# Moving a kernel's own DRAM traffic from SyncE's queue to GpSimd's, in a two-layer hybrid encoder

## The chip, the cores and the metric

The kernel runs on one core of a Trainium2 chip. A core has the engines TensorE (PE, its weight loads PEld), VectorE (DVE), ScalarE (ACT), GpSimd (POOL) and SyncE (SP), and sixteen DMA engines that move data between DRAM and the on-chip memory. Each engine works its own instruction list in order and waits on semaphores for the others; a DMA is issued by an instruction on one engine and runs on the DMA engines. The metric is the device time of one execution in microseconds, as the median of several runs.

## The reference

Two layers run over 256 tokens of 1024 channels (float32). Cut to what matters:

```python
h = rmsnorm(x, norm1_g[l])
rq, rk, rv, rg, c_q, c_kv, k_rope, s5_u, gate_logits = split(h @ w_in[l])
y_ret = retention(rq, rk, rv, rg)              # A: 4 heads, both directions
y_mla = latent_attention(c_q, c_kv, k_rope)    # B: 8 heads, softmax over 256 keys
y_s5  = glu(gelu(s5(s5_u) + d * s5_u) @ w_glu) # C: 64 groups x 64 complex states, both directions
proj  = einsum('bsnk,nkd->bsnd', stack(y_ret, y_mla, y_s5), w_branch[l])
x = x + sum(sigmoid(gate_logits) * proj) @ w_out[l]
x = x + (silu(f_gate) * f_up) @ ffn_w_down[l]  # f_gate, f_up from rmsnorm(x) @ ffn_w_gu[l]
```

After the second layer there is a final RMSNorm.

## The kernel before, in words

Activations are held with channels on the partitions. A dense product takes its weights as tiles `raw` of up to 128 x 1024 numbers, 512 KB each, out of five buffers (`wraw`). ScalarE rounds each into `wh` (L668), VectorE takes the rest `wl` = `raw` - `wh` (L669), and TensorE makes three matmuls for each 128-row block (L673, L674, L675; L713 to L715 for the GLU). Some of the first products use `raw` as it is (L725).

The S5 branch is a generator (`s5`) that runs in the background of the dense work: after each weight tile, `tick` gives it some credit, and it emits a few steps. The order in which the engines execute is then set by a planner which takes instructions from each engine's list by priority, once their inputs are ready by its own estimate of times. So the place of an instruction on an engine depends on how long the planner thinks that earlier DMAs take.

On-chip memory is short, and so the kernel keeps much of its own data in DRAM (tiles from the pool `dr`) and fetches it again: the powers `pxd`, the input factors `bbd`, sixteen state tables `wtd` in layer 1, transposed inputs and states `utd`, `sfd`, `sbd`, some gates `gd`, the skip term `dud`, the residual `xd`. One use is more than storage. In `s5_out` a product of 128 x 480 numbers, `kf`, is stored to `kd`, and four loads read it back as overlapping windows of 128 (steps of 16 numbers), one load of 128 KB for each group `g4`, into the tile `M` (tag `wt`, two buffers). This happens once for every two values of the loop's `qq`, eight times in a layer. Here it is called a round: ScalarE copies `kf` (L598), a store, four loads, then the matmuls of L629 in `s5_emit`, which take `M` as weights. `s5_emit` comes one step later in the program than the store (`delay`=1).

All of these transfers, like the loads of weights and inputs, go through one helper, `dma` (L121), which issues them on SyncE. GpSimd has only memsets: the last 16 columns of the tile `t_bb` (L365), two columns of the state tiles (L472, L473), parts of other tiles.

Of the kernel before, what the change touches and what calls it, by code (L numbers as in the profile page):

```python
# [78 lines left out]
class Kern:  # L79
# [40 lines left out]
    def dma(self, out, src, pin=False):  # L120
        i = self.nc.sync.dma_start(out, src)  # L121
        if self.pin or pin:
            self.tc.keep_in_program_order(i)
        return i

    def s4(self, dt=F32):
        return self.s(1024, "s4", dt=dt)
# [161 lines left out]
    def s5_tables(self, l):  # L289


        nc, V, A = self.nc, self.nc.vector, self.nc.scalar
        pn, cf = yield from self.s5_params(l)
        yield 4.0
        PX = self.s4().rearrange("p (j d g) -> p j d g", j=8, d=2)
        for b in range(2):
            ps = self.bank(self.p5)
            for j in range(4):
                nc.tensor.matmul(ps[:, j * P:(j + 1) * P], pn[:, b * 4 + j].rearrange("p r q -> p (r q)"),
                                 self.perm, start=True, stop=True)  # L300
            A.copy(PX[:, b * 4:b * 4 + 4].rearrange("p j d g -> p (j d g)"), ps)
        CF = self.s(2 * 64, "t_cf").rearrange("p (r g) -> p r g", r=2)
        ps = self.bank(self.p5)
        nc.tensor.matmul(ps[:, 0:P], cf.rearrange("p r q -> p (r q)"), self.perm, start=True, stop=True)
        for r in range(2):
            for d in range(2):
                A.copy(CF[d * 64:d * 64 + 64, r, :], ps[r * 64:r * 64 + 64, d * 64:d * 64 + 64])
        PW = self.s4().rearrange("p (r s g) -> p r s g", r=2, s=8)
        A8 = self.s(2 * 64, "t_a8").rearrange("p (r g) -> p r g", r=2)
        A8s = self.s(2 * 64, "t_a8s").rearrange("p (r g) -> p r g", r=2)  # L310
        for r in range(2):
            nc.gpsimd.memset(PW[0:64, r, 0, :], 1.0 - r)
            nc.gpsimd.memset(PW[64:128, r, 7, :], 1.0 - r)
            rows = slice(r * 64, r * 64 + 64)
            A.copy(PW[0:64, r, 1:8, :], PX[rows, 0:7, 0, :])
            A.copy(PW[64:128, r, 6::-1, :], PX[rows, 0:7, 1, :])
        for d in range(2):
            rows = slice(d * 64, d * 64 + 64)
            A.copy(A8[rows, 0, :], PX[0:64, 7, d, :])
            A.copy(A8[rows, 1, :], PX[0:64, 7, d, :])  # L320
            A.mul(A8s[rows, 0, :], PX[64:128, 7, d, :], -1.0)
            A.copy(A8s[rows, 1, :], PX[64:128, 7, d, :])
        PXD = self.t(self.dr, [P, 1024], "pxd", 2)
        self.dma(PXD, PX.rearrange("p j d g -> p (j d g)"))
        if l == 0 and self.nl >= 0:
            while "b" not in self.cx:
                yield None
            br, bi = self.cx.pop("b")
        else:
            br, bi = self.s4(), self.s4()  # L330
            for f in self.load_b(l, br, bi):
                f()
        BB = [self.s4(), self.s4()]
        for qh in range(2):
            c = slice(qh * 512, qh * 512 + 512)
            nat = lambda t: t[:, c].rearrange("p (h q c) -> p h q c", h=4, q=8)
            natt = lambda t: t.rearrange("p (h q c) -> p h q c", h=4, q=8)
            cfv = lambda r: (CF[:, r, qh * 32:qh * 32 + 32].rearrange("p (q h) -> p h q", h=4)
                             .unsqueeze(3).to_broadcast([P, 4, 8, GC]))
            for r, (x, y, op) in enumerate(((br, bi, ALU.subtract), (bi, br, ALU.add))):  # L340
                yield 1.9
                t1, t2 = self.s(512, "tm"), self.s(512, "tm")
                V.tensor_tensor(natt(t1), cfv(0), nat(x), ALU.mult)
                V.tensor_tensor(natt(t2), cfv(1), nat(y), ALU.mult)
                V.tensor_tensor(BB[r][:, c].rearrange("p (q h c) -> p h q c", q=8, h=4), natt(t1), natt(t2), op)
        BBD = self.t(self.dr, [P, 2048], "bbd", 2)
        for r in range(2):
            self.dma(BBD[:, r * 1024:(r + 1) * 1024], BB[r])
        PD = self.s(512, "t_pd").rearrange("p (s g) -> p s g", s=8)
        V.tensor_tensor(PD, PW[:, 1], PW[:, 0], ALU.subtract)  # L350
        V.scalar_tensor_tensor(PW[:, 1], PW[:, 1], -1.0, PW[:, 0], ALU.mult, ALU.subtract)
        BS = self.s4()
        V.tensor_tensor(BS, BB[0], BB[1], ALU.add)
        return dict(PW=[PW[:, 0], PW[:, 1], PD], PXD=PXD, A8=A8, A8s=A8s, BB=[BS, BB[1], BB[0]], BBD=BBD)

    def s5_out_tables(self, l, tb, qh):
# [3 lines left out]
        BB2 = self.s(2 * 528, "t_bb2", 1).rearrange("p (d x) -> p d x", d=2)  # L360
        for d in range(2):
            for r in range(2):
                self.dma(BB2[r * 64:r * 64 + 64, d, 0:512],
                                  tb["BBD"][d * 64:d * 64 + 64, r * 1024 + qh * 512:r * 1024 + qh * 512 + 512])
            nc.gpsimd.memset(BB2[:, d, 512:528], 0.0)  # L365
        AB = self.s4().rearrange("p (k d j g) -> p k d j g", k=2, d=2, j=8)
        gs = slice(qh * 32, qh * 32 + 32)
        PX = self.s(512, "ev").rearrange("p (j d g) -> p j d g", j=8, d=2)
        self.dma(PX, tb["PXD"].rearrange("p (j d g) -> p j d g", j=8, d=2)[:, :, :, gs])
        gs = slice(0, 32)  # L370
        for d in range(2):
            js = slice(0, 8) if d == 0 else slice(7, None, -1)
# [27 lines left out]
    def s5(self, l, ctx, gel_out):  # L400
# [4 lines left out]
        wtd = None  # L405
        if l > 0:
            wtd = []
            for qq in range(16):
                wt = yield from self.s5_wt(tb, qq)
                d = self.t(self.dr, [P, 1024], "wtd", 16)  # L410
                self.dma(d, wt)
                wtd.append(d)
                yield self.yw / 2 if self.fw else self.yw
            tb.pop("PW"), tb.pop("BB")
# [26 lines left out]
        for qq in range(16):  # L441
            if wtd is None:
                wt = yield from self.s5_wt(tb, qq)
            else:
                wt = self.s(1024, "wt")
                self.dma(wt, wtd[qq])
            WT = wt.rearrange("p (g r x) -> p g r x", g=4, r=2)
            if qq % 2 == 0:
                pl = self.bank(self.p5)
# [51 lines left out]
        for t, k in ((UT, "utd"), (Sf, "sfd"), (Sb, "sbd")):  # L501
            d = self.t(self.dr, [P, 1024], k, 2)
            v = t.pop()
            self.dma(d, v if len(v.shape) == 2 else v.rearrange("p a b -> p (a b)"))
            t.append(d)
        del v
        tb.update(UT=UT, Sf=Sf, Sb=Sb)
# [33 lines left out]
    def s5_out(self, l, tb, du_load, gel_out):  # L541
        nc, V, A, T = self.nc, self.nc.vector, self.nc.scalar, self.nc.tensor
        pend = todo = None
        for qq in range(16):
            qh, q = qq // 8, qq % 8
            if q == 0:
                BB2, C1, C2, AB = yield from self.s5_out_tables(l, tb, qh)
                yq = self.s4().rearrange("p (t q c) -> p t q c", t=8, q=8)
                UT, Sf, Sb = (tb[k][qh] for k in ("UT", "Sf", "Sb"))
                if qh:  # L550
                    ts = []
                    for d in (UT, Sf, Sb):
                        t = self.s4()
                        self.dma(t, d)
                        ts.append(t)
                    UT = ts[0].rearrange("p (q x) -> p q x", q=8)
                    Sf, Sb = (t.rearrange("p (g n) -> p g n", n=32) for t in ts[1:])
                yield 1.0
# [38 lines left out]
            kf = self.s(512, "ev")[:, 0:480]  # L597
            A.copy(kf, pk[:, 0:480])  # L598
            kd = self.t(self.dr, [P, 480], "kd", 4)
            self.dma(kd, kf)  # L600
            M = self.s(1024, "wt").rearrange("p (h q m) -> p h q m", h=4, q=2)
            for g4 in range(4):
                base = kd[g4 * 32:g4 * 32 + 16, :]
                src = bass.AP(tensor=base.tensor, offset=base.offset, ap=[[16, 8], [480, 16], [240, 2], [1, 128]])
                self.dma(M[:, g4].rearrange("p q m -> p (q m)"), src)
            job = (list(pend), M, po, yq, UT, Sf, Sb, qh, q)
            pend = None
            if self.delay:
# [567 lines left out]
    def gate(self, l, n, h, c):  # L1176
        th = self.s(512, "ev")
        if (n, c) in self.gd:
            self.dma(th, self.gd.pop((n, c)))
            return th  # L1180
        pg = yield from self.pair_steps(self.a["w_in"][l], OFF_GATE + n * D + c * 256, h.get)
        self.nc.scalar.activation(th, pg, AF.Tanh, scale=0.5)
# [2 lines left out]
    def early_gates(self, l, h, ns):  # L1185

        for n, c in ns:
# [1 line left out]
                continue  # L1189
            th = yield from self.gate(l, n, h, c)  # L1190
            self.gd[n, c] = self.t(self.dr, [P, 512], "gd", 12)
            self.dma(self.gd[n, c], th)

    def branch(self, l, n, y, c):
        return self.pair_steps(self.a["w_branch"][l, n], c * 256, y.get)
# [1 line left out]
    def layer(self, l, x2, acc, xg, last):  # L1197
# [28 lines left out]
        for qh in range(2):  # L1226
# [11 lines left out]
                                 scale=sd[:, k:k + 1])  # L1238
            dus.append(du)
            if not (l == 0 and self.nl >= 0):  # L1240
                self.dma(dud[:, qh * 1024:(qh + 1) * 1024], du)
        while self.loads:
            self.load()
        if l == 0 and self.nl >= 0:
            for qh in range(2):
                self.dma(dud[:, qh * 1024:(qh + 1) * 1024], dus[qh])
        del du, dus
        xd = self.t(self.dr, [P, 2048], "xd", 1)
        for i in range(2):
            self.dma(xd[:, i * 1024:(i + 1) * 1024], x2[i])  # L1250
        cx = self.cx
        gel = []

        def du_load(qh):
            t = self.s4()
            self.dma(t, dud[:, qh * 1024:(qh + 1) * 1024])
            return t

        def gel_out(qh, y):
# [65 lines left out]
        acc = self.squares(2 * S)  # L1325
        x2 = [self.s4(), self.s4()]
        for i in range(2):
            self.dma(x2[i], xd[:, i * 1024:(i + 1) * 1024])
        g2 = self.vec["norm2_g"][l]
        h2 = self.hl(2)  # L1330
        for c in range(4):
# [168 lines left out]
```

## Time and profile before

| | |
|---|---|
| median of 3 runs | 1427.78 us (1423.44 to 1439.42) |
| profiled execution, its time | 1425.45 us |
| profiled execution, its span | 1423.5 us |
| mean granted clock of TensorE | 0.982 |
| PE, DVE, ACT, POOL busy | 94%, 73%, 57%, 0% of the span |
| DMA, read and written | 231.53 MB and 27.53 MB |

The profile is one execution. The span goes from the first to the last instruction; the time has 1.95 us more around it. The three runs lie within 16 us, 1.1% of the median.

### The profile page before, as it was taken

The numbers are of one execution on the slowest core, as the hardware profiler recorded it, in microseconds if no ns is written. First come the engines' busy times: TensorE is split into PE (matmuls) and PEld (weight loads), VectorE is DVE, ScalarE is ACT, GpSimd is POOL, SyncE is SP. The second block draws the span as 40 slices with busy tenths as digits, with TensorE's granted clock in tenths as the row PEclk, the third lists the DMA queues.
The fourth block names the chain that finished last, engine by engine and source line by source line (L and its number), as shares of the span: only waits on it lengthen the run. The fifth ranks groups of instructions, "written<-read, shape, count | busy, mean of one in ns | idle before, by whom it ended". The sixth has DMA issues, their size and how long they took to land.

```text
span 1423.5 us, 27613 instructions
## 1 busy us (share of the span) xinstructions
PE 1334.4 (94%) x11102; PEld 1234.2 (87%) x11102; DVE 1042.3 (73%) x1910; ACT 807.0 (57%) x1339; POOL 4.5 (0%) x33
## 2 busy tenths in 40 slices
PE   7899998888999999999999999788999999999997
PEld 5866878867888999999999868778988899999997
DVE  7977867877687679988668547877768657777754
ACT  3656576974654455545446677786564344544442
POOL 0000000000000000000000000000000000000000
PEclk9999999999999999999999999999999999999999
DMA  8944233646786699766679784365687667666662
GB/s 218 250 146 118 69 104 99 182 137 152 211 219 194 201 211 260 210 199 197 188 229 273 239 267 131 99 193 156 157 247 188 193 200 204 181 185 187 179 179 79
DMA packets 433891, 260.84 MB, mean 183 GB/s; under 512 B 61714, under 2 KB 413284, under 8 KB 433764
## 3 DMA queue, kind: packets, MB, share of 16 engines
q1 hardware_dynamic: 433764, 259.09, 64.3%
q8 instruction: 87, 1.43, 0.4%
q14 instruction: 40, 0.33, 0.1%
HBM read 231.53 MB, written 27.53 MB: 182 GB/s over the span
## 4 chain that ended last, share of the span: by engine, by line
PE 68%; ACT 13%; DMA 8%; DVE 6%; issue 3%; SPq 1%; DVEq 0%; ACTq 0%
PE pw L673 17%; PE pw L674 17%; PE pw L675 17%; DMA wt<-kd 3%; ACT wh L668 3%; PE pw L713 2%; PE pw L714 2%; PE pw L715 2%; DVE wl L669 2%; DMA kd<-ev 2%; ACT s L497 2%; PE p L536 2%; PE p L452 2%; DMA raw<-in_w_in 1%; SPq L121 1%
## 5 line engine op out<-in xcount | busy, mean ns | idle before, releaser
L673 PE MATMUL pw<-s,wh 128*128 128x256 f32 x2472 | 714.6, 290 | 16.6 <-ACT wh L668 13.8
L675 PE MATMUL pw<-s,wl 128*128 128x256 f32 x2472 | 703.5, 285 | 8.4 <-DVE wl L669 8.3
L674 PE MATMUL pw<-s,wh 128*128 128x256 f32 x2472 | 703.0, 285 | 0.2 <-DVE s L749 0.2
L668 ACT CAST wh<-raw 128x1024 fp32r<-128x1024 f32 (+4 forms) x394 | 381.0, 972 | 456.2 <-PE pw L674 290.7
L669 DVE TENSOR_TENSOR wl<-raw,wh 128x1024 fp32r<-128x1024 f32 (+4 forms) x394 | 443.1, 1128 | 206.8 <-ACT wh L668 205.4
L673 PEld LDWEIGHTS pw<-s,wh 128*128 128x128 f32 x2472 | 472.1, 191 | 34.1 <-ACT wh L668 16.6
L675 PEld LDWEIGHTS pw<-s,wl 128*128 128x128 f32 x2472 | 472.5, 191 | 15.5 <-DVE wl L669 11.2
L674 PEld LDWEIGHTS pw<-s,wh 128*128 128x128 f32 x2472 | 472.9, 191 | 6.6 <-issue 4.8
L713 PE MATMUL pw<-s,wh 128*128 128x256 f32 x256 | 71.9, 281 | 0.0
L714 PE MATMUL pw<-s,wh 128*128 128x256 f32 x256 | 71.9, 281 | 0.0
L715 PE MATMUL pw<-s,wl 128*128 128x256 f32 x256 | 71.9, 281 | 0.0
L569 DVE TENSOR_TENSOR wy<-s,s 128x512 f32<-128x512 f32 x64 | 42.3, 687 | 16.1 <-PE pa L629 10.3
L715 PEld LDWEIGHTS pw<-s,wl 128*128 128x128 f32 x256 | 48.2, 188 | 0.0
L714 PEld LDWEIGHTS pw<-s,wh 128*128 128x128 f32 x256 | 48.2, 188 | 0.0
L713 PEld LDWEIGHTS pw<-s,wh 128*128 128x128 f32 x256 | 48.2, 188 | 0.0
L536 PE MATMUL p<-ident,wy 128*128 128x128 f32 x256 | 36.7, 276 | 11.5 <-ACT s L468 11.1
L497 ACT COPY s<-s 64x256 f32<-64x256 f32 (+1 forms) x64 | 40.7, 636 | 5.2 <-DVE s L483 4.3
L536 PEld LDWEIGHTS p<-ident,wy 128*128 128x128 f32 x256 | 28.6, 140 | 16.6 <-ACT s L468 13.2
L570 DVE TENSOR_TENSOR tm<-s,s 128x512 f32<-128x512 f32 x64 | 43.0, 687 | 0.0
L571 DVE TENSOR_TENSOR wy<-wy,tm 128x512 f32<-128x512 f32 x64 | 42.7, 685 | 0.0
L748 ACT ACTIVATE s<-ev 128x512 fp32r<-128x512 f32 x46 | 29.1, 633 | 19.7 <-DVE ev L1350 12.1
L531 DVE TENSOR_TENSOR wy<-wy,tm 128x1024 f32<-128x1024 f32 x32 | 39.1, 1221 | 0.3
(284 smaller groups left out, 1549.7 us busy)
## 6 DMA issues: line engine op xcount, KB each, us to landing
raw<-in_w_in SPq DMA_DIRECT2D x122, 512.0 KB
raw<-in_ffn_w_gu SPq DMA_DIRECT2D x88, 512.0 KB
raw<-in_w_branch SPq DMA_DIRECT2D x48, 512.0 KB
raw<-in_s_w_glu SPq DMA_DIRECT2D x32, 512.0 KB
raw<-in_ffn_w_down SPq DMA_DIRECT2D x32, 512.0 KB
wt<-kd SPq DMA_DIRECT2D x64, 128.0 KB
raw<-in_w_out SPq DMA_DIRECT2D x16, 512.0 KB
wtd<-wt SPq DMA_DIRECT2D x16, 512.0 KB
```

The lines of the kernel that those rows point to most:

```text
L497: A.copy(*todo.pop(0))
L536: T.transpose(ps[:, i * P:(i + 1) * P], W[i % 2][:, gp * 2 + i // 2].rearrange("p s c -> p (s c)"), self.ident)
L570: V.tensor_tensor(t2, tv(1), cv(C2), ALU.mult)
L571: V.tensor_tensor(y[:, :, js, :], y[:, :, js, :], t2, ALU.add)
L668: self.nc.scalar.copy(hi, src)
L669: self.nc.vector.tensor_tensor(lo, src, hi.bitcast(F32), ALU.subtract)
L673: T.matmul(ps, lh, rh, start=first, stop=False)
L674: T.matmul(ps, lh, rl, start=False, stop=False)
L675: T.matmul(ps, ll, rh, start=False, stop=last)
L713: T.matmul(o, wh[:, k, c], xh, start=(half == 0 and m == 0 and k == 0), stop=(k == 3), **f)
L714: T.matmul(o, wh[:, k, c], xl, start=False, stop=(k == 3), **f)
L715: T.matmul(o, wl[:, k, c], xh, start=False, stop=(k == 3), **f)
```

## The change

A new helper `park` issues a transfer on GpSimd's queue. Every store of the kernel's own data to DRAM and every load of it back calls `park` in place of `dma`. Loads of inputs, weights and constant tables, and the stores of the output, stay with `dma` on SyncE. The tiles, their buffers and the compute instructions are the same.

```diff
+    def park(self, out, src):
+
+        return self.nc.gpsimd.dma_start(out, src)
...
-        self.dma(PXD, PX.rearrange("p j d g -> p (j d g)"))
+        self.park(PXD, PX.rearrange("p j d g -> p (j d g)"))
...
-            self.dma(BBD[:, r * 1024:(r + 1) * 1024], BB[r])
+            self.park(BBD[:, r * 1024:(r + 1) * 1024], BB[r])
...
-                self.dma(BB2[r * 64:r * 64 + 64, d, 0:512],
+                self.park(BB2[r * 64:r * 64 + 64, d, 0:512],
                                   tb["BBD"][d * 64:d * 64 + 64, r * 1024 + qh * 512:r * 1024 + qh * 512 + 512])
...
-        self.dma(PX, tb["PXD"].rearrange("p (j d g) -> p j d g", j=8, d=2)[:, :, :, gs])
+        self.park(PX, tb["PXD"].rearrange("p (j d g) -> p j d g", j=8, d=2)[:, :, :, gs])
...
-                self.dma(d, wt)
+                self.park(d, wt)
...
-                self.dma(wt, wtd[qq])
+                self.park(wt, wtd[qq])
...
-            self.dma(kd, kf)
+            self.park(kd, kf)
...
-                self.dma(M[:, g4].rearrange("p q m -> p (q m)"), src)
+                self.park(M[:, g4].rearrange("p q m -> p (q m)"), src)
```

In the same way: the stores and loads of `utd`, `sfd`, `sbd`, `gd`, `dud` and `xd`.

## Rows read from the trace of the kernel before

**Rows 1.** The page, busy time and share of the span by engine:

```profile
PE 1334.4 (94%) x11102; PEld 1234.2 (87%) x11102; DVE 1042.3 (73%) x1910; ACT 807.0 (57%) x1339; POOL 4.5 (0%) x33
```

**Rows 2.** Waits, all engines: who waited for what, total us, times, longest us:

```profile
PEld pa L629 <- DMA wt<-kd: 17.5, 23, 1.3
...
PE pa L629 <- DMA wt<-kd: 11.3, 19, 1.1
...
PE p L452 <- DMA wt<-wtd: 1.6, 2, 1.1
...
DVE s L642 <- DMA s<-dud: 2.0, 2, 1.1
...
SPq L121 <- DVE wl L669: 607.7, 228, 10.4
SPq L121 <- ACT ev L598: 48.1, 13, 10.8
...
SPq L121 <- DMA kd<-ev: 23.7, 15, 3.8
```

**Rows 3.** Stretches around rounds and near the start: busy us by engine, clock, DMA:

```profile
325.80:339.00 13.20, 10.21 (x118) 8.45 (x119) 8.58 (x12) 7.34 (x14) 0.00 (x0) 1.00 0.55 135
...
1015.00:1033.00 18.00, 18.00 (x201) 16.57 (x194) 14.49 (x23) 10.41 (x23) 0.00 (x0) 1.00 0.69 174
1033.00:1047.00 14.00, 14.00 (x116) 13.18 (x116) 6.10 (x9) 6.70 (x15) 0.16 (x2) 1.00 0.78 205
...
sum 234.50, PE 222.09 PEld 195.26 DVE 167.92 ACT 117.09 POOL 1.68; mean PE 12.34 PEld 10.85 DVE 9.33 ACT 6.50 POOL 0.09
...
51.00:57.00 6.00, 3.26 (x25) 3.05 (x26) 6.00 (x10) 4.97 (x8) 0.00 (x0) 1.00 1.18 298
57.00:62.00 5.00, 3.96 (x32) 3.55 (x32) 5.00 (x7) 4.20 (x7) 0.00 (x0) 1.00 0.97 308
```

**Rows 4.** Chain in order of time, pieces of five rounds: start us, us, what:

```profile
311.37 2.00 DMA kd<-ev
...
313.39 0.66 SPq L121
...
315.35 5.68 DMA wt<-kd
...
326.40 4.36 DMA kd<-ev
...
424.11 3.44 DMA wt<-kd
...
1040.28 5.21 DMA ev<-pxd
...
1117.42 2.53 DMA kd<-ev
...
1121.90 4.67 DMA wt<-kd
```

**Rows 5.** Tiles `kd`, `bbd`: issues, ns min/median/max, first and last start us:

```profile
L121 SPq DMA_DIRECT2D wt<-kd x64: 569/577/1268, 313.4 to 1121.9; - x64
...
L121 SPq DMA_DIRECT2D t_bb<-bbd x16: 444/541/1489, 62.5 to 1039.6; - x16
```

**Rows 6.** SyncE in order of time, near the start and at 1040 us:

```profile
36.26 0.52 SPq L121 DMA_DIRECT2D pxd<-s  x1
...
43.12 2.58 SPq L121 DMA_DIRECT2D dud<-s  x1
45.81 8.48 SPq L121 DMA_DIRECT2D raw<-in_w_in  x5
...
1040.28 0.60 SPq L121 DMA_DIRECT2D ev<-pxd  x1
```

**Rows 7.** GpSimd in order of time, with the idle time before and its releaser:

```profile
780.54 0.17 POOL L472 MEMSET s<- 128x32 f32 x1 [346.84 <-PE pw L674]
```

**Rows 8.** DMA queues: the queue of all kernel transfers, its packets, MB, share:

```profile
q1 hardware_dynamic: 433764, 259.09, 64.3%
```

**Rows 9.** VectorE by form: count, busy us, mean ns, idle before:

```profile
L669 DVE TENSOR_TENSOR wl<-raw,wh 128x1024 fp32r<-128x1024 f32 x330 | 403.0, 1223 | 192.1 <-ACT wh L668 191.1 <-DMA raw<-in_w_in 0.2
...
L938 DVE SCALAR_TENSOR_TENSOR at<-pa,at 128x512 f32<-128x512 f32 x8 | 5.5, 690 | 7.5 <-ACT at L933 7.5
...
L931 DVE TENSOR_SCALAR at<-s,lg 128x512 f32<-128x512 f32 x8 | 3.9, 482 | 0.5 <-DMA s<-in_rel 0.5
```

More of the change, by code (lines that the diff above doesn't have):

```diff
@@ L503, in s5 @@
             v = t.pop()
-            self.dma(d, v if len(v.shape) == 2 else v.rearrange("p a b -> p (a b)"))
+            self.park(d, v if len(v.shape) == 2 else v.rearrange("p a b -> p (a b)"))
             t.append(d)
@@ L553, in s5_out @@
                         t = self.s4()
-                        self.dma(t, d)
+                        self.park(t, d)
                         ts.append(t)
@@ L1178, in gate @@
         if (n, c) in self.gd:
-            self.dma(th, self.gd.pop((n, c)))
+            self.park(th, self.gd.pop((n, c)))
             return th
@@ L1191, in early_gates @@
             self.gd[n, c] = self.t(self.dr, [P, 512], "gd", 12)
-            self.dma(self.gd[n, c], th)
+            self.park(self.gd[n, c], th)
     def branch(self, l, n, y, c):
@@ L1240, in layer @@
             if not (l == 0 and self.nl >= 0):
-                self.dma(dud[:, qh * 1024:(qh + 1) * 1024], du)
+                self.park(dud[:, qh * 1024:(qh + 1) * 1024], du)
         while self.loads:
@@ L1245, in layer @@
             for qh in range(2):
-                self.dma(dud[:, qh * 1024:(qh + 1) * 1024], dus[qh])
+                self.park(dud[:, qh * 1024:(qh + 1) * 1024], dus[qh])
         del du, dus
@@ L1249, in layer @@
         for i in range(2):
-            self.dma(xd[:, i * 1024:(i + 1) * 1024], x2[i])
+            self.park(xd[:, i * 1024:(i + 1) * 1024], x2[i])
         cx = self.cx
@@ L1255, in du_load @@
             t = self.s4()
-            self.dma(t, dud[:, qh * 1024:(qh + 1) * 1024])
+            self.park(t, dud[:, qh * 1024:(qh + 1) * 1024])
             return t
@@ L1327, in layer @@
         for i in range(2):
-            self.dma(x2[i], xd[:, i * 1024:(i + 1) * 1024])
+            self.park(x2[i], xd[:, i * 1024:(i + 1) * 1024])
         g2 = self.vec["norm2_g"][l]
```

## Prediction

> **What bounds the kernel now.** I read the page first. TensorE is busy 1334.4 us of the span [rows 1], so 89 us (1423.5 - 1334.4) is all that better transfers could ever give back. Next come the waits, for who ends those idle times [rows 2]: of the transfers that the change moves, one kind stands out, the loads of `M` out of `kd`, for which the matmuls of L629 wait 11.3 us (their weight loads 17.5 us, largely the same time). The loads of `wtd` cost TensorE 1.6 us, those of `dud` cost VectorE 2.0 us; `gd`, `xd` and the states end none of the waits that I list. SyncE's own waits [rows 2] show who holds the issuer back: 607.7 us for VectorE's `wl`, which is waiting for a free `raw` buffer, against 48.1 us for the copy `kf` and 23.7 us for a store of `kd` to land. SyncE has time to spare, and weights are requested as early as five buffers allow. Then I took the stretches around the sixteen rounds [rows 3]: TensorE is idle 12.4 us in them (234.50 - 222.09), very unevenly: 3.0 us in the stretch from 325.8 us, none in that from 1015 us. So what a round costs depends on where the planner put L629 behind its loads. Last, the chain in order of time [rows 4]: nine of the sixteen rounds stand in it, the first at 311 us, the last at 1117 us. In those nine, a round that takes 1 us longer stops TensorE 1 us longer, since it works in order.
>
> **What moves.** 194 of SyncE's issues go to GpSimd: 64 loads of `M` and 16 stores of `kd`, 32 of `wtd`, 28 of `gd`, 16 of `xd` and `dud`, 20 of `bbd`, 6 of `pxd`, 12 of states; by the sizes in the code 57 MB of the queue's 259.09 [rows 8]. Bytes, DMA engines and compute instructions stay the same, so the change acts through three things: how long an issue takes, who stands ahead in a queue, and the order.
>
> **The rounds.** A round in the chain is: store lands, three further issues, last load lands. In the first it is 2.00 us, then three issues of about 0.65 us (the first of them 0.66), then 5.68 us [rows 4], with L629 starting 9.7 us after the copy. In the nine rounds of the chain the store takes 3.07 us in the mean (2.00 to 4.36), the last load 4.84 us (3.44 to 5.68).
>
> The trace has no transfer issued by GpSimd, so its price is bounded by SyncE's issues. At the lower end GpSimd issues like SyncE, 577 ns [rows 5]: nothing is added. I see no reason for it to be faster, but a tenth of a microsecond less can't be excluded and would give 0.5 us a round. At the upper end I take the longest issue of `t_bb`, 1489 ns [rows 5], 0.9 us more. I take +0.5 us, nearer to the longest issue of the same load, 1268 ns (+0.69), than to the median, because a 128 KB load out of `kd` is cut into 256 pieces whoever writes them. Five issues in a round follow one another (store, then four loads, each visible in the arrival of the last), so 5 x 0.5 = +2.5 us.
>
> The Trainium skill, page "DMA: Bandwidth & Descriptors", section "Specifications", puts the first byte at about 1 us from GpSimd and about 0.6 us from SyncE. No row here shows GpSimd's side; by that price the estimate would be 5 x 0.4 = +2.0 us a round in place of +2.5.
>
> Against this stands the queue. Now a store or load stands behind the weight tiles that SyncE issued before it; I read the spread of 2.00 to 4.36 us for the same 240 KB store, and of 3.44 to 5.68 us for the last load, as that. With a queue of its own it no longer does, but it still shares the sixteen engines, whose share is 0.55 to 0.69 in such stretches [rows 3]. All of the excess over the shortest is 1.07 + 1.40 = 2.5 us a round; none of it is the other bound. I take half, -1.2 us.
>
> So a round gets 2.5 - 1.2 = 1.3 us longer, and nine of them 12 us. The planner gives part of that back: where L629 lies behind more other matmuls, as in seven rounds of sixteen, the round is covered, and it places L629 by the latencies that it expects of this queue. It can do that well or not at all; I take half: **+6 us**. Bounds: with no added issue time and all of the queue's excess gone, a round is 2.5 us shorter, which can't give back more than the idle time there, **-12 us**; with 0.9 us an issue, no relief and no help from the order, 9 x 4.5 = **+40 us**.
>
> **The change of half at 1037 to 1046 us.** Here four loads of `t_bb`, the store of `kd` and the load of `pxd` follow each other at 0.5 to 0.6 us each, and the load of `pxd` then stands in the chain with 5.21 us [rows 4, 6]. Six issues at +0.5 us make its landing 3 us later. What hides it is TensorE's dense work, busy 14.00 us of 14.00 there [rows 3]; if that cover is gone, it costs the whole 3 us, and the same once more in layer 0. I take **+2 us** (0 to +6).
>
> **The start.** Between 36 and 46 us a store of `pxd` and one of `dud`, 1 MB together, are queued ahead of five weight tiles on SyncE, the latter held 2.58 us in its issue; the tiles then take 8.48 us to issue [rows 6]. Right after, TensorE is idle 2.74 us of 6.00 and 1.04 us of 5.00 [rows 3]. On another queue the stores no longer stand ahead of the tiles, though their bytes still go through the same engines, which are full there (share 0.97 to 1.18). Of the 3.8 us I take **-3 us** (0 to -4).
>
> **Edits at nothing.** SyncE's waits for `kf` and the landed stores, 72 us, move to GpSimd; TensorE gains nothing by it, because five `raw` buffers cover it (SyncE itself waits 607.7 us for a free one) [rows 2]. `wtd`, `gd`, `xd`, `dud` and the states are wanted long after they are issued, or by engines with idle time; the cover is the dense matmuls, and without it the most that the rows show is 0.9 us added on each of the sixteen loads of `wtd`, 14 us, of which TensorE now waits 1.6 us [rows 2].
>
> GpSimd gets in-order waits of its own: the loads of `M` wait for their store, and `gd`, `dud` and state transfers queue behind them. Behind a memset it can be worse: before the one at 780.54 us GpSimd had stood 346.84 us [rows 7]. It had nothing else to do then, so this shows a late release and not a blocked queue; if a `wtd` store stood behind such a memset, its `wt` buffer would stay taken and the copies into it would stop. I take nothing, since the planner orders GpSimd's list by readiness too.
>
> **The sum.** +6 + 2 - 3 = +5 us on the profiled execution, 1425.45 to 1430.5 us. The median is 2.3 us above that execution, so I add the 5 us to 1427.8: **1433 us**.
>
> **The rivals.**
> - *The round becomes the limit.* GpSimd takes 0.8 us or more longer for an issue, five stand in a row, and TensorE stops at L629 in nine rounds or more: 1427.8 + 40 = **1468 us**. For it: the nine rounds have no slack now, and GpSimd has issued nothing in this trace. Against it: the queue's relief, up to 2.5 us a round. It decides from about +0.8 us an issue (5 x 0.8 - 1.2 = 2.8 us a round, 25 us in nine).
> - *Relief wins.* Transfers that no longer stand behind weight tiles come sooner than the longer issue costs: -12 in the rounds, -3 at the start, **1413 us**. For it: the spread of the same store from 2.00 to 4.36 us. Against it: at most 12.4 us of idle time are there to win.
> - *VectorE holds GpSimd up.* Each issue in a round waits for the VectorE instruction that runs. VectorE is busy 73% [rows 1], with instructions of 690 to 1223 ns [rows 9]: half of 1223 ns times 0.73 is 0.45 us an issue, 5 x 9 x 0.45 = 20 us on top of the forecast, **1453 us**. The rows can't show it, as GpSimd issues nothing now. The Trainium skill, page "SBUF — State Buffer", section "SBUF: two separate sides", says that a VectorE instruction in a two-port mode locks GpSimd out, so that it can't write the descriptors of its DMAs. By that rule the trace speaks against this rival: the one-source form at L931 takes 482 ns for 512 columns and only 3.9 us in all, while the forms that fill VectorE's time have two sources and take 690 ns for as many [rows 9].
> - *The order alone.* The planner's new times move other work, with no transfer slower: 10 us either way. That a transfer stays on SyncE is no rival: each of the 194 goes through the new helper.
>
> **How the numbers follow.** About 1% (14 us) is what a measurement here can tell from no change: the three runs span 16 us. Chances: forecast, with the reordering in it, 0.58; round as limit 0.24; relief 0.12; VectorE 0.06. Faster by over 1% (below 1413.5) is half of relief and a little of the forecast's low side, 0.08. Slower by over 1% (above 1442) is the first and third rival and a little of the high side, 0.31. The rest, 0.61, is within 1%. The range goes from 1415 us, near all of the relief, to 1464 us, just short of the worst bound of the rounds; outside are the tails of both, about 0.2.
>
> **What would show it.** Right: GpSimd shows some 194 transfers; L629's waits for `kd` stay between 5 and 30 us; stretches without rounds keep their times; stores of `kd` land in 2 to 3 us. Wrong: L629's waits of 40 us and more, with the gap between issues of one round's loads above 1.4 us (first rival), or gaps that end with VectorE instructions (third). It would be wrong altogether if TensorE's idle time grew outside the rounds, in the loads of `wtd` or behind a GpSimd memset.

## The result, and the profile after

The changed kernel takes **1501.18 us** in the median of four runs (1489.26 to 1509.74) against 1428.37 us before: the ratio is 1.0493, 95% interval 1.0398 to 1.0587. I had forecast 1433 us and a range that ended at 1464 us. The profiled execution after took 1500.2 us, its span is 1498.4 us, and 0.959 of TensorE's full clock was granted, against 0.982 before.

The page after, busy time by engine and the queues:

```profile
PE 1369.0 (91%) x11102; PEld 1259.6 (84%) x11102; DVE 1043.8 (70%) x1910; ACT 807.4 (54%) x1339; POOL 136.5 (9%) x227
...
PEclk9999999988998999999999999999998899999999
...
q1 hardware_dynamic: 391492, 201.67, 50.1%
q0 software_dynamic: 18976, 57.49, 12.2%
```

Read against [rows 1], this page divides the loss. The span grew by 74.9 us. TensorE's idle time went from 89.1 to 129.4 us (1498.4 - 1369.0), **+40.3 us**; its busy time went from 1334.4 to 1369.0 us, **+34.6 us**, for the same 11102 matmuls. So nearly half of the loss is not waiting at all: the same work ran slower. The clock accounts for it: 0.041 of 1498.4 us less 0.018 of 1423.5 us is 35.8 us of full speed lost. The row of the clock shows where: in the slices at 300 to 375, 450 to 487 and 1124 to 1199 us, all of which hold rounds. The 57 MB moved as expected [rows 8].

The waits after:

```profile
PEld pa L633 <- DMA wt<-kd: 56.3, 35, 3.6
...
PE pa L633 <- DMA wt<-kd: 45.8, 31, 3.4
...
PE p L456 <- DMA wt<-wtd: 5.4, 2, 3.9
...
DVE s L646 <- DMA s<-dud: 3.3, 1, 3.3
```

(L633 is L629 of before; the helper moved the lines by four.) Against [rows 2], TensorE's waits for `M` grew from 11.3 us in 19 waits to 45.8 us in 31: 34.5 of the 40.3 us of new idle time. Of these, 24.7 us came in the nine rounds of the chain before (11.3 us there, now 36.0) and 9.7 us in the seven others, in which TensorE had not waited at all; six of the seven now have a wait. `wtd` adds 3.8 us.

GpSimd's issues of the tile `kd`, and two of its other loads; then the chain in order of time, the first store and the fourth loads that stand in it:

```profile
L128 POOL DMA_DIRECT2D wt<-kd x64: 917/920/956, 316.0 to 1193.2; - x64
L128 POOL DMA_DIRECT2D kd<-ev x16: 542/570/580, 313.5 to 1187.6; - x16
```

```profile
L128 POOL DMA_DIRECT2D t_bb<-bbd x16 | 8.5, 539 | 39.0 <-PE p L588 22.1 <-DMA bbd<-s 16.8
...
L128 POOL DMA_DIRECT2D ev<-pxd x4 | 4.7, 1181 | 12.9 <-DVE wl L673 12.1 <-issue 0.8
```

```profile
313.50 2.25 DMA kd<-ev
...
1053.38 8.11 DMA wt<-kd
...
1072.90 7.63 DMA wt<-kd
...
1152.74 7.38 DMA wt<-kd
```

An issue of a load of `M` takes 920 ns against SyncE's 577 [rows 5], so +0.34 us, less than the +0.5 us I had taken. But the fourth load, which in the nine rounds of the chain before had landed in 4.84 us in the mean [rows 4], now takes 6.4 us in the same nine. The chain after shows only three of its fourth loads (in other rounds the wait that counts is for an earlier load), so here and below I take each load's landing from the last update of its semaphore in the trace, in all sixteen rounds. From the store's issue to the first load's issue it is 3.71 us in the mean, against 3.03 us before; from the first to the fourth issue 2.77 against 2.00; from the fourth issue to its landing 6.63 (4.2 to 8.4) against 4.99 (4.3 to 6.9). A round is thus 3.1 us longer, 13.1 in place of 10.0 us: 0.7 up to the first load, 0.8 by three further issues, 1.6 by the landing. Its store is issued some 0.3 us later behind the copy as well.

What SyncE sends meanwhile has changed too. Between the store's issue and the fourth load's, it had sent 10 weight tiles in the sixteen rounds together, none of them among the four loads. After, it sends 31, 14 of them among the loads.

The last round shows what that does to TensorE. Stretches of 2 us of the kernel before, then of the kernel after (busy us by PE, PEld, DVE, ACT, POOL with counts in brackets, granted clock, DMA share, GB/s):

```profile
1120.00:1122.00 2.00, 2.00 (x19) 2.00 (x18) 0.82 (x1) 0.06 (x1) 0.00 (x0) 1.00 0.81 262
1122.00:1124.00 2.00, 1.47 (x10) 0.86 (x10) 0.77 (x1) 1.04 (x1) 0.00 (x0) 1.00 0.58 166
1124.00:1126.00 2.00, 2.00 (x12) 1.29 (x12) 0.45 (x1) 0.00 (x0) 0.00 (x0) 1.00 1.04 239
```

```profile
1192.00:1194.00 2.00, 0.75 (x7) 0.55 (x5) 0.85 (x1) 1.05 (x1) 2.00 (x3) 1.00 1.08 320
1194.00:1196.00 2.00, 0.00 (x0) 0.00 (x0) 0.38 (x1) 0.00 (x0) 1.26 (x3) 0.89 1.03 145
1196.00:1198.00 2.00, 1.83 (x7) 1.08 (x7) 0.00 (x0) 0.00 (x0) 0.00 (x0) 0.50 1.00 175
1198.00:1200.00 2.00, 2.00 (x9) 1.16 (x7) 0.00 (x0) 0.00 (x0) 0.00 (x0) 0.50 1.05 359
1200.00:1202.00 2.00, 2.00 (x25) 1.71 (x28) 0.00 (x0) 0.00 (x0) 0.00 (x0) 0.50 0.79 302
```

Before, TensorE stood for 0.5 us and the granted clock stayed at 1.00. After, it stood for 3.4 us, the granted clock fell to 0.50 (1.2 in place of 2.4 GHz), and three stretches are "busy" at half speed: the wait is paid a second time in part. Single matmuls show it too, in ns min/median/max, before and after:

```profile
L629 PE MATMUL pa<-wt,s x256: 272/273/297, 318.1 to 1127.4; 128*32 128x128 f32 x128
```

```profile
L633 PE MATMUL pa<-wt,s x256: 272/297/423, 322.2 to 1202.5; 128*32 128x128 f32 x128
```

### The profile page after: what moved, and what is told of

It reads as the page before. It is cut to its first block, busy times and chain, and to the rows that moved or that the text cites. A ratio compares the mean times of both kernels' runs of the same rounds, so it can differ in the third digit from the quotient of the medians.

```text
span 1498.4 us, 27705 instructions
## 1 busy us (share of the span) xinstructions
PE 1369.0 (91%) x11102; PEld 1259.6 (84%) x11102; DVE 1043.8 (70%) x1910; ACT 807.4 (54%) x1339; POOL 136.5 (9%) x227
## 3 DMA queue, kind: packets, MB, share of 16 engines
q1 hardware_dynamic: 391492, 201.67, 50.1%
q0 software_dynamic: 18976, 57.49, 12.2%
## 4 chain that ended last, share of the span: by engine, by line
PE 57%; issue 12%; DMA 11%; ACT 10%; DVE 6%; POOL 2%; SPq 2%; DVEq 0%; POOLq 0%; ACTq 0%
PE pw L677 14%; PE pw L678 14%; PE pw L679 14%; DMA wt<-kd 3%; ACT wh L672 2%; DMA kd<-ev 2%; DVE wl L673 2%; PE pw L717 2%; PE pw L719 2%; PE pw L718 2%; POOL wt L128 2%; PE p L456 2%; ACT s L501 2%; SPq L121 2%; PE p L540 1%
## 5 line engine op out<-in xcount | busy, mean ns | idle before, releaser
L677 PEld LDWEIGHTS pw<-s,wh 128*128 128x128 f32 x2472 | 478.4, 194 | 34.7 <-ACT wh L672 15.2
L679 PEld LDWEIGHTS pw<-s,wl 128*128 128x128 f32 x2472 | 478.1, 194 | 10.9 <-DVE wl L673 6.0
L678 PEld LDWEIGHTS pw<-s,wh 128*128 128x128 f32 x2472 | 478.8, 194 | 9.0 <-issue 5.0
L633 PE MATMUL pa<-wt,s 128*32 128x128 f32 x256 | 38.9, 341 | 46.0 <-DMA wt<-kd 45.8
L573 DVE TENSOR_TENSOR wy<-s,s 128x512 f32<-128x512 f32 x64 | 42.3, 687 | 40.3 <-PE pa L633 31.7
L633 PEld LDWEIGHTS pa<-wt,s 128*32 128x32 f32 x256 | 18.3, 133 | 59.1 <-DMA wt<-kd 56.3
L128 POOL DMA_DIRECT2D wt<-kd x64 | 59.0, 926 | 42.3 <-DMA kd<-ev 33.8
L718 PEld LDWEIGHTS pw<-s,wh 128*128 128x128 f32 x256 | 48.2, 188 | 0.0
L719 PEld LDWEIGHTS pw<-s,wl 128*128 128x128 f32 x256 | 48.2, 188 | 0.0
L717 PEld LDWEIGHTS pw<-s,wh 128*128 128x128 f32 x256 | 48.2, 188 | 0.0
```

Source lines behind the costliest of these rows:

```text
L128: return self.nc.gpsimd.dma_start(out, src)
L633: T.matmul(po[g4 * 32:g4 * 32 + 32, oc:oc + 128], lhsT, rhs, start=(k == 0), stop=(k == 2), tile_position=(0, g4 * 32))
L677: T.matmul(ps, lh, rh, start=first, stop=False)
L678: T.matmul(ps, lh, rl, start=False, stop=False)
L679: T.matmul(ps, ll, rh, start=False, stop=last)
L717: T.matmul(o, wh[:, k, c], xh, start=(half == 0 and m == 0 and k == 0), stop=(k == 3), **f)
```

## The experiments

Two theories. **Sharing**: SyncE works in order, so in the kernel before, while it stands for a store of `kd`, few weight tiles go out; the round has the engines more to itself. On any other queue the round meets more of the weights. **GpSimd's own path**: the issues and what lies behind them take longer, whoever else is sending. Times of before beside the runs were 1430.27 us (e1 to e4), 1431.83 (e5 to e8), 1434.3 (e9, e10) and 1428.46 (e11 to e13).

**Which of the moved transfers costs it: e1 to e4.** e1 is the changed kernel with the round's five transfers back on SyncE; e2, e3 and e4 are the kernel before with only the round moved, only its loads, only its store:

```diff
 e1:  self.dma(kd, kf)     self.dma(M[:, g4]..., src)    # all others: park
 e2:  self.park(kd, kf)    self.park(M[:, g4]..., src)   # all others: dma
 e3:  self.dma(kd, kf)     self.park(M[:, g4]..., src)
 e4:  self.park(kd, kf)    self.dma(M[:, g4]..., src)
```

> The changed kernel with the rounds alone (16 stores of kd and 64 loads of M) back on SyncE, the other 114 transfers on GpSimd. Theory 1, the rounds carry the loss: 1420 to 1436 us, the waits of L633 for M back to 8 to 16 us. Theory 2, the other transfers, queued in order on GpSimd, carry it: 1480 us or more.

> The kernel before with the rounds alone on GpSimd, the other 114 transfers on SyncE. Theory 1: 1485 to 1510 us, waits for M of 40 us or more and a lower granted clock in the rounds. Theory 2: 1425 to 1440 us.

> The kernel before with the 64 loads of M alone on GpSimd, the stores of kd on SyncE. If the loads are the slow part of a round (they land 5.5 to 8 us after the last issue, the stores in 2.3 to 4.7): 1475 to 1505 us. If the five software issues in a row are what costs, four of five are left: 1475 to 1490 us as well, but the gap from store to first load stays under 0.5 us and the loads' spacing of 0.92 us explains the stall by itself. If the store is the slow part: 1430 us.

> The kernel before with the 16 stores of kd alone on GpSimd. If the loads carry the loss: 1420 to 1435 us, perhaps a little faster, since the store no longer stands behind weight tiles. If any transfer issued by GpSimd in the chain costs as much as another: a fifth of the 73 us, some 1440 us.

Measured: e1 1449.9 us, ratio 1.0132 (1.0093 to 1.0171); e2 1498.12, 1.0467 (1.0432 to 1.0502); e3 1477.4, 1.0321 (1.0282 to 1.0359); e4 1438.74, 1.0054 (1.0038 to 1.0070). TensorE's waits for `M` are 14.9, 46.5, 34.8 and 16.6 us. So 80 of the 194 transfers make 4.7 of the 4.9%, the 64 loads most of it. The stores alone cost 0.5%, so they are not the relief that e4's first expectation had. The other 114, which I had at nothing but for the change of half and the start, cost 1.3% alone, so neither theory of e1 holds as it stands. (The two don't add up: 6.0 against 4.9%.)

The same four runs give the clock's price. Against the profile before, TensorE's added idle and added busy time are 4.3 and 9.7 us (e4), 14.5 and 12.6 (e1), 28.7 and 24.7 (e3), 37.5 and 35.8 (e2), 40.3 and 34.6 (the change). For the large ones 0.86 to 0.95 us of slower work come with each us of idling; in the runs below it is 0.60 (e8) to 0.82 (e9). Small differences say nothing here: e7, as fast as the kernel before, has 1339.1 us of busy time, 4.7 more than the profile of before.

**Another queue that isn't GpSimd's: e5.** The kernel before, with the loads of `M` issued by ScalarE:

```diff
-                self.dma(M[:, g4].rearrange("p q m -> p (q m)"), src)
+                nc.scalar.dma_start(M[:, g4].rearrange("p q m -> p (q m)"), src)
```

> The kernel before with the 64 loads of M issued by ScalarE: a queue of their own, as GpSimd's is, but issued in hardware, as SyncE's are. The time itself is muddied, since ScalarE stands for each store to land (2 to 4 us a round, up to 50 us of its time in all): 1430 to 1460 us. What is to be read is the landing: if a queue of its own brings relief, as the prediction had it, the loads land in 3.0 to 3.5 us against 5.7 from GpSimd; if they share the DMA engines as badly as GpSimd's do, 5 us or more.

1456.36 us, ratio 1.0165 (1.0126 to 1.0205); waits for `M` 21.4 us. ScalarE's issues take 597 ns in the median, as SyncE's do, so half of e3's 3.2% comes without any slower issue. What the run was to show is the landing. Four fourth loads from its chain:

```profile
338.09 4.12 DMA wt<-kd
...
1039.37 6.77 DMA wt<-kd
...
1092.94 7.92 DMA wt<-kd
...
1113.16 6.95 DMA wt<-kd
```

In all sixteen rounds it is 6.4 us in the mean, near GpSimd's 6.6 and not SyncE's 5.0: a queue of its own brings no relief, and the landing gets longer without GpSimd. SyncE sends 23 weight tiles in these rounds, 10 of them among the loads. For the time it isn't a pure test: ScalarE, in order as well, now stands idle 29.3 us while its four issues wait for the store (10.4 + 8.6 + 4.6 + 3.5 + 2.2). TensorE's wait for its casts `wh` did not grow by it (11.8 us, 13.8 before).

**Fewer pieces: e6 and e7.** `kf` is written interleaved, so that a load of `M` is 128 pieces of 1 KB and not 256 of 512 B; e6 in the changed kernel, e7 in the kernel before:

```diff
-            A.copy(kf, pk[:, 0:480])
+            A.copy(kf.rearrange("p (x q) -> p q x", q=2), pk[:, 0:480].rearrange("p (q x) -> p q x", q=2))
...
-                src = bass.AP(..., ap=[[16, 8], [480, 16], [240, 2], [1, 128]])
+                src = bass.AP(..., ap=[[32, 8], [480, 16], [1, 256]])
```

> The changed kernel with kf written with the two values of q side by side, so that a load of M has 128 runs of 1 KB in place of 256 of 512 B; the same bytes, the same five transfers a round. If the number of pieces sets both GpSimd's issue (0.92 us) and the landing (5.7 us): issues of 0.55 us, landings of 3 to 4 us, 1440 to 1465 us. If the landing is set by bytes that share the engines with the weight tiles: only the issues get shorter, 1485 to 1497 us.

> The same layout in the kernel before, all on SyncE. If pieces count there as well: the waits for M go from 11 us to under 4 us, 1410 to 1422 us, faster than before. If not: 1424 to 1432 us.

e6: 1476.23 us, ratio to before 1.0315 (1.0277 to 1.0353); e7: 1431.36, 1.0002 (0.9979 to 1.0025). GpSimd's issue falls with the pieces, from 920 to 616 ns in the median:

```profile
L128 POOL DMA_DIRECT2D wt<-kd x64: 587/616/655, 313.2 to 1168.4; - x64
```

The median landing falls from 5.9 to 5.1 us and the waits for `M` from 45.8 to 31.9 us. So GpSimd's time per piece is a real part, some 25 us of the 73; 3% stay when its issue is nearly as short as SyncE's. In the kernel before the same layout is worth nothing: SyncE's issue takes 568 ns in the median for 128 pieces and 577 for 256, and the waits for `M` are 12.2 us, 11.3 before.

**More cover: e8 and e10.** A round's results are taken 1.5 us later by the planner's count, which was to put some 24 more dense matmuls (of weight tiles) between a round's store and its first matmul on `M`; e8 in the changed kernel, e10 in the kernel before:

```diff
             if todo is not None:
+                yield 1.5
                 yield from self.s5_emit(todo, du_load, gel_out)
```

> The changed kernel with a pause of 1.5 us of the background's credit before each s5_emit, which puts some 24 dense matmuls (2.9 us at full clock) more between the copy kf and L633 in most rounds; no transfer is changed. If the loss is TensorE's stop at L633 and what the clock loses by it: the waits fall from 46 us to 15 to 30 us, and the time to 1455 to 1480 us. If the transfers cost by contention with the weight tiles, cover doesn't help: 1495 us or more.

> The kernel before with the one line of e8 (a round's results are taken 1.5 us later by the planner's count, so that some 24 more dense matmuls lie between a round's store and its first M matmul). If too little cover is what the rounds suffer from in both kernels, the waits for M fall from 11.3 to 4 to 7 us and the time to 1415 to 1425 us. If the planner's delay merely moves the dense work, so that later rounds have less, the time is 1425 to 1440 us.

e8: 1492.64 us, ratio 1.0408 (1.0369 to 1.0447), waits 36.6 us; its time can't be told from the changed kernel's, whose interval begins at 1.0398. e10: 1453.28 us, 1.0131 (1.0116 to 1.0146), waits 15.8 us, with a single wait of 4.5 us among them. The edit doesn't do the same in every round. In twelve rounds of e8 there are 4 to 47 more dense matmuls between the copy and the first matmul on `M`, and the waits there fall from 39.1 to 15.7 us. In four (the last of each layer, and one more in each) there are 14 to 21 fewer, and the waits grow from 6.7 to 20.9 us. In e10 it is the same: 9.3 to 3.5 us in the twelve, 2.0 to 12.3 us in the four. So cover does shorten the stops where it is given, but with this edit matmuls that are put into one place are missing in another. Whether another order covers all sixteen rounds was not tried.

**Take the weights out of the round: e9.** The changed kernel, in which SyncE must wait for `M` before it goes on:

```diff
+            hold = self.t(self.dr, [P, 64], "hold", 4)
+            self.dma(hold[0:1, 0:16].rearrange("p (h x) -> p h x", h=4), M[0:1, :, 0, 0:4], pin=True)
```

> The changed kernel, with one more SyncE transfer in each of the 16 rounds: 64 bytes of the loaded M are sent to DRAM, so that SyncE, which works in order, cannot issue the next weight tiles before all of M has landed. All of the computation is kept. Theory A (sharing: GpSimd's loads are late because SyncE, which no longer stands in the round, sends weight tiles alongside): loads land in about 4 us instead of 5.9, waits of TensorE for M fall from 45.8 us to 15 to 25, PE busy falls below 1355 us, and the time is 1440 to 1465 us, if the later weights cost less than that. Theory B (GpSimd's four issues of 0.92 us and its path are slow by themselves): landing stays above 5.3 us, waits at 38 to 46, time 1490 to 1510 us.

1492.83 us, ratio 1.0418 (1.0399 to 1.0436), which can't be told from the changed kernel's either. By the time and by the median landing, 5.4 us, this is theory B's outcome; the waits lie between the two:

```profile
PE pa L635 <- DMA wt<-kd: 35.4, 30, 3.1
```

10 us fewer, not 20 to 30. The edit does only part of what it was to do. In nine rounds one or two weight tiles still stand ahead of the hold in SyncE's list and go out among the loads; there the fourth load lands in 6.4 us in the mean, 7.1 in the same rounds of the changed kernel. In the seven rounds in which none goes out among them, it lands in 4.6 us against 6.0 (5.1 in the kernel before). In the last of these the first matmul on `M` starts 3.6 us after the first load's issue (1179.97 to 1183.60), as against 5.7 in the changed kernel and 3.0 before. So the sharing is there, and where the tiles are held its cost is gone. But the tiles held back then go out in a bunch around the next store, and store to first load is 3.87 us (mean of 16), longer than without the hold. SyncE in order of time, and GpSimd, at the last rounds:

```profile
1171.62 0.59 SPq L121 DMA_DIRECT2D hold<-wt  x1
1172.31 7.09 SPq L121 DMA_DIRECT2D raw<-in_s_w_glu  x3
```

```profile
1175.87 0.58 POOL L128 DMA_DIRECT2D kd<-ev  x1 [7.07 <-ACT ev L602]
...
1179.97 3.67 POOL L128 DMA_DIRECT2D wt<-kd  x4 [3.52 <-DMA kd<-ev]
```

**The round by itself: m0 and m1.** Two small kernels that run only chained rounds, each ending in one VectorE operation on all of `M`; m0 with nothing beside them, by three issuers in turn, m1 with weight tiles on SyncE and two issuers in turn:

```python
getattr(self, "on_" + path)(kf, kd, m)      # store and four loads by path: sync, scalar (m0 only), gpsimd
nc.vector.tensor_tensor(kf, m[:, 0:480], m[:, 544:1024], ALU.add)
```

> Leaves out the whole computation; only chained rounds run (store of 128x480, four M loads, one VectorE operation on all of M), 8 of them by each issuer, SyncE, ScalarE and GpSimd, with no weight traffic. Theory A (sharing): GpSimd's loads land in 2.5 to 3.5 us, and its round is only 1.5 to 2 us longer than SyncE's, by four issues of 0.92 instead of 0.58 us. Theory B (GpSimd's path is slow by itself): its loads land in 5 us or more here too, and its round is 4 us or more longer than SyncE's.

> The same rounds, by SyncE and GpSimd in turn, with four weight tiles of 512 KB issued by SyncE for each; the computation is left out. Theory A: a SyncE round is as long as in the quiet kernel or up to 1.5 us longer, since SyncE issues no weight tile between its store and its loads; a GpSimd round that has weight tiles in flight is 2 to 4 us longer than its quiet one, and its loads land in 5 us or more. Theory B: both grow by the same amount.

VectorE's waits for the three in m0, total of eight rounds; GpSimd's issues there; and, from the page, KB and us from issue to landing:

```profile
DVE kf L103 <- DMA mgpsimd<-kdgpsimd: 75.2, 8, 9.8
DVE kf L100 <- DMA mscalar<-kdscalar: 64.0, 8, 8.5
DVE kf L97 <- DMA msync<-kdsync: 63.4, 8, 8.3
```

```profile
L94 POOL DMA_DIRECT2D mgpsimd<-kdgpsimd x32: 919/920/938, 25.1 to 219.0; - x32
```

```profile
mgpsimd<-kdgpsimd POOLq DMA_DIRECT2D x32, 128.0 KB, 3.5
```

Alone, a round takes 7.9 us from SyncE, 8.0 from ScalarE and 9.4 from GpSimd: its own path costs **1.5 us a round**, and its loads land in 3.5 us (median), where the page of the changed kernel has 5.9:

```profile
wt<-kd POOLq DMA_DIRECT2D x64, 128.0 KB, 5.9
```

Its parts there, in the mean of eight rounds, from the store's issue: 2.7 us to the first load, 2.8 to the fourth, 3.6 until VectorE starts, against 2.0, 1.9 and 4.0 from SyncE and 2.0, 2.0 and 4.0 from ScalarE. So in quiet GpSimd's round takes 1.6 us more up to the fourth load and 0.4 less behind it, 1.2 us from the store's issue on; the other 0.3 pass before that issue. In the kernel the stretch up to the fourth load grew by about the same, 1.5 us, but the landing got 1.6 us longer and not shorter. What the kernel shows beyond the path, 1.9 us a round (3.1 against 1.2), comes from the company.

In m1 both rounds grow by about the same, to 11.0 us (SyncE, 88.2/8) and 13.0 us (GpSimd, 104.2/8). That is what theory B of m1 had, and both halves of theory A missed: SyncE's round grew by 3.1 us and not by up to 1.5, and GpSimd's loads landed in 3.4 us (median) and not in 5 or more. In order of time it is plain why:

```profile
64.13 6.03 SPq L72 DMA_DIRECT2D raw<-in_ffn_w_gu  x4
82.89 0.34 SPq L85 DMA_DIRECT2D kdsync<-kf  x1
83.33 1.14 SPq L72 DMA_DIRECT2D raw<-in_ffn_w_gu  x2
85.12 2.90 SPq L86 DMA_DIRECT2D msync<-kdsync  x4
```

```profile
69.85 0.58 POOL L93 DMA_DIRECT2D kdgpsimd<-kf  x1 [14.38 <-DVE kf L97]
76.04 3.66 POOL L94 DMA_DIRECT2D mgpsimd<-kdgpsimd  x4 [5.61 <-DMA kdgpsimd<-kf]
```

SyncE's store has its first load 2.23 us after it (2.0 in m0): the tiles come behind the store, and two of them ahead of the loads, from whose first issue it is 8.2 us to VectorE's operation (93.36), 5.9 in m0. GpSimd's store meets four tiles that SyncE has just sent, and its first load is issued 6.2 us after it, against 2.6 in m0; with the tiles gone, the loads then take 6.2 us (to 82.21), no longer than in m0 (6.4). A queue of its own didn't take the store past the weights. And m1 doesn't copy the kernel: here tiles go out between SyncE's store and its loads in every round, two in most, where the kernel before sent 10 in sixteen rounds.

**The other 114: e11, e12 and e13.** The kernel before with one group each on GpSimd: `wtd`; `gd` and `xd`; the tables, states and `dud`:

```diff
 e11:  self.park(d, wt)    self.park(wt, wtd[qq])                      # all others: dma
 e12:  self.park(th, self.gd...)    self.park(self.gd[n, c], th)    self.park(xd..., x2[i])    self.park(x2[i], xd...)
 e13:  self.park(PXD, ...)  ... (BBD, ...)  (BB2, ...)  (PX, ...)  (UT, Sf, Sb)  (dud, ...)  (t, dud...)
```

> The kernel before with only the spill of the second layer's tiles on GpSimd: 16 stores to wtd and 16 loads of wt from it. All of the computation is kept. Theory C (the 1.3% of e1 comes from loads that are waited for, and the second layer's loads of wt are the ones that TensorE reaches soonest): 1437 to 1447 us, with 4 to 6 us of TensorE's waits on wt<-wtd instead of 1.6. Theory D (the cost is the order of SyncE's list, which is spread over all groups): 1430 to 1436 us, as for each of the three groups. The forecast had priced this group at nothing: 1426 to 1432 us.

> The kernel before with only gd (12 gate tiles of a layer out and back) and xd on GpSimd. All of the computation is kept. Theory C: nothing waits for these closely, 1427 to 1433 us. Theory D: 1430 to 1436 us. Forecast: no change, 1426 to 1432 us.

> The kernel before with only the tables, the states and dud on GpSimd (pxd, bbd, utd, sfd, sbd, dud and their loads): nine lines of the change. All of the computation is kept. Theory C: 1430 to 1437 us, since the loads of the states and of ev<-pxd, with 2048 pieces, precede each half's rounds, and the wait of TensorE for s_c_im grows from the front of SyncE's list. Theory D: 1430 to 1436 us. Forecast: 0 to -1 us, 1426 to 1432 us.

e11: 1432.26 us, 1.0030 (0.9999 to 1.0060); e12: 1431.11, 1.0024 (1.0000 to 1.0047); e13: 1439.59, 1.0084 (1.0054 to 1.0113). The three add up to 1.4%, as e1 has it. The first two are nothing that I can tell from no change. e13 is not, and its loss lies at the two changes of half: stretches of before, then of e13:

```profile
350.00:400.00 50.00, 47.17 (x487) 41.26 (x489) 31.70 (x47) 32.10 (x61) 0.77 (x4) 1.00 0.80 211
1050.00:1100.00 50.00, 46.74 (x516) 41.73 (x515) 42.69 (x60) 29.37 (x52) 0.00 (x0) 1.00 0.82 226
```

```profile
350.00:400.00 50.00, 44.50 (x418) 37.94 (x417) 27.31 (x41) 26.18 (x53) 6.11 (x13) 0.93 0.70 192
1050.00:1100.00 50.00, 41.73 (x400) 37.73 (x399) 32.48 (x47) 29.99 (x57) 2.66 (x5) 0.93 0.74 207
```

In layer 0 the copies of `kf` on either side of the change of half are 29.3 us apart (363.42, 392.76) and were 23.6 us (363.14, 386.73). The DMA share is lower, not higher: the loads come later, they don't crowd. Part of that is SyncE's own list. TensorE waits 6.4 us for `s_c_im`, 0.6 us before, and in layer 1 SyncE issues these four loads from 1057.0 us on, 9.9 us after that round's store (1047.14), where before it was 5.8 us (1038.55, 1044.4):

```profile
PE p L393 <- DMA s<-in_s_c_im: 6.4, 2, 5.4
```

Why the list shifts so was not tried; the wait for `s_c_im` also grew in e5 and e10 (5.1 and 4.1 us), which move none of these transfers.

## Why the prediction was wrong

- **What bounds the kernel, and where the change would act: right.** The loads of `M` are what TensorE waits for, and the rounds make 4.7 of the 4.9% (e2).
- **The issue, +0.5 us: mis-sized, in the safe direction.** GpSimd takes 0.34 us more for a load of `M` and 0.23 more for the store, together 1.6 us for the five instead of 2.5; m0 gives the whole path 1.5 us. (The 9.7 us after the copy that the prediction names for L629 run to the fourth load's landing; its first matmul on `M` started 6.8 us after the copy, at 318.12 us.) I had put the price on the pieces, and e6 bears that out. The Trainium skill, page "DMA: Bandwidth & Descriptors", section "Specifications", led to 2.0 us, nearer than my own term; neither decided the result.
- **The queue's relief, -1.2 us a round: the step that failed first.** It has the wrong sign. I read the spread of landings as time behind weight tiles in SyncE's queue, and concluded that another queue escapes them. But the order of SyncE's list also kept tiles back while it stood for a store, and I had seen those 23.7 us [rows 2] and booked them as a wait that nobody needs. Excess was there: a round from SyncE takes 10.0 us in the kernel and 7.9 alone. (It was a little less than the 2.5 us that I had read: the shortest landing, 3.44 us, isn't a fourth load's, which took 4.6 us in that round.) But on GpSimd's queue the fourth load takes 1.6 us longer, while SyncE sends 31 tiles in the rounds in place of 10. e5 shows the same landing on a queue whose round alone (8.0 us) is no longer than SyncE's, m0 that GpSimd's loads land in 3.5 us without company, m1 a store stuck among tiles, e9 that the landing comes back in the rounds where the tiles are held. A round grew by 3.1 us where I had 1.3.
- **"The planner gives part back", half of 12 us: didn't happen.** TensorE's order is the same in all but 112 of its 11102 matmuls, and the number of dense matmuls between a round's copy and its first matmul on `M` is unchanged, within 3, in every round. So nothing was given back, and the seven rounds that I had as covered were covered by less than the round grew: they add 9.7 us of waits, the nine in the chain 24.7, which is 2.7 us each. e8 and e10 show that cover can be given, there at the price of other rounds.
- **The clock: not in the sum at all.** I treated a stall as costing its own length. In the rounds before, waits of at most 1.1 us for `M` had left the clock at 1.00; waits of up to 3.4 us, two or more in many rounds, brought it to 0.50, and 34.6 us of slower matmuls lie on top of 40.3 us of idling. Even the worst bound, +40 us, had only the idling, and the span grew by 35 us more. That the bound comes so near the 40.3 us is luck: it put 4.5 us on each of nine rounds, which got 2.7.
- **The change of half, +2 us (0 to +6): mis-sized.** In e13, with the rounds on SyncE, it is 5.8 us in layer 0, and all of that group costs 0.84%, 12 us.
- **The start, -3 us: not seen.** In the two stretches of [rows 3] TensorE is idle 3.7 us after, 3.8 us before, has done 41 matmuls in place of 57, and the clock is lower:

```profile
51.00:57.00 6.00, 2.28 (x16) 1.88 (x16) 5.97 (x10) 2.52 (x3) 0.00 (x0) 0.87 1.18 291
57.00:62.00 5.00, 5.00 (x25) 5.00 (x25) 5.00 (x7) 2.78 (x7) 1.59 (x3) 0.50 1.06 308
```

- **Edits at nothing.** For `wtd`, `gd` and `xd` right within some half per cent (e11, e12). The tables, states and `dud` were not nothing (e13). No wait behind a memset shows.
- **The rivals.** "The round becomes the limit" named the right place and the right sign (waits of 45.8 us), but by another mechanism: it wanted issues 0.8 us longer, and GpSimd's are 0.34. "Relief wins" falls with the step above. "VectorE holds GpSimd up" falls: 64 issues take 917 to 956 ns beside a VectorE that is busy 70%, and 919 to 938 ns in m0, where it has almost nothing to do. "The order alone" falls with TensorE's order, which hardly changed.

How much of a round's 3.1 us is GpSimd's path (1.2 us by m0, counted from the store's issue) and how much the company (the rest) is an estimate by difference. The two don't add simply in the whole kernel: e6 takes away 1.8%, and e9 10 us of the waits but no time that can be told, both less than their theory had. Why the change of half gets longer in e13 is open too. No version here beats the kernel before; e7, e11 and e12 can't be told from it.

## What to carry to other kernels

Before a dependent round trip is taken off an in-order queue, ask what that order keeps away from it: an issuer that stands for the store also holds back the prefetches that would share the engines with the loads. Where TensorE has no slack behind such a trip, price the added idle time of such stalls at more than its length, here 1.6 to 1.95 times, because the matmuls behind it run at the lower clock. And cost the whole trip by itself first, quiet and beside the real traffic; the issue time alone explained less than half.

## What the runs showed of the hardware

- GpSimd's time for an issue rises with the pieces, but not in proportion: 0.54 us (median) for the loads of `t_bb` in 64 pieces, 0.62 us for 128 (e6), 0.92 us for 256, 1.18 us (mean) for the 2048 of `ev<-pxd`. SyncE's issue of a load of `M` takes 0.58 us in the median for 256 pieces and 0.57 for 128 (e7).
- After a stall of 3.4 us TensorE's granted clock was 0.50 for about the next 6 us of matmuls, though they followed one another; after one of 0.5 us it stayed at 1.00.
- Beside the weights, the fourth load of a round lands in 6.4 us from ScalarE (e5) and 6.6 us from GpSimd, 5.0 us from SyncE, whose own list keeps most tiles out of the round. Alone (m0) it is no slower from the other two.
- Beside the weights' 201.67 MB, GpSimd's 128 KB loads land in 5.9 us (median); alone they take 3.5 us.
